# Where the splits of the next weights stand around the conditional part behind the last pair of experts

## The chip, the cores and the metric

The kernel runs on one core of a Trainium2 chip. The metric is the time of one execution on the device in microseconds, the median of the runs made; lower is better.

## What is computed

The reference is one transformer block with a mixture of experts, followed by two layers of a second kind. Cut to what stands around the change:

```python
h2 = rmsnorm(x, norm_ffn_g).reshape(b * s, d)          # 512 tokens, d = 1024
m = hierarchical_moe(h2, ...)                          # 2 of 32 experts for each token
x = rmsnorm(x + m, final_norm_g)                       # end of the first block

# second block, for l = 0, 1
h = rms_norm(x, norm_gain[l])
cols = h @ w_in                                        # layer 0: w_in_a (q, k, v, q_mem, gate)
kv = rms_norm(mem, mem_gain) @ w_mem_kv[l]             # memory: 256 rows, keys and values of layer l
```

## The kernel before

**The experts.** The 32 experts run as 16 pairs (a loop over j at L1468). For each pair 64 token slots are gathered for either expert, turned (`turn_tokens`), multiplied with the gate and up weights (`gate_up`, L1405), activated (`hidden`, L1410 to L1412), turned (`turned`, L1418 to L1420) and multiplied with the down weights (`down`, L1431). The output `y` leaves its two banks in halves: ScalarE copies the first (L1435), VectorE the second (L1433). GpSimd then scatters `y` into the DRAM tensor `yd` (L1436).

**The conditional part.** An expert with more than 64 tokens needs an extra pass. `extra(e)` (L1504) is written 14 times under nested conditions (L1549) on a count that is read at run time. With these data the count is zero and every engine branches over all 14 passes. Behind the branch each engine makes an entry on its own semaphore (and SP and GpSimd on those of their DMAs) for what the skipped code would have counted; in the trace these are the instructions of L1549 that are called EVENT_SEMAPHORE and INC_SWDGE_SEM. What another engine does behind the branch on a bank that the skipped code also uses waits for that entry.

**What follows.** `x2` holds four chunks of 128 tokens. To each, two tiles `m` read back from `yd` (L1563, L1564) are added (`add_experts`, L1566, L1567). TensorE transposes the chunks (`transposed`): chunk by chunk into six banks (three called sc, one oT, two tp) at L404, and then the last two slabs of 128 columns at L412 into sc banks that the first slabs have left. ScalarE and VectorE turn each slab into a pair `hh`, `hl` (L383, L384). Then the first projection of the new rows starts (`natural`, matmuls `sc<-whi,hh`). Besides, `square` (L1571) sums the squares of a chunk, `gF2` (L1559) is the squared gain, and both are used for the scale `R` of the rows.

**The fill.** The keys and values of the memory for layer 1 (`vB_steps` with `memory_steps`, and `mem_k`) need nothing of the experts. They are given to TensorE piece by piece (`pump`) around the additions and transposes. `mT` is the transposed memory, loaded by `mem_load` and split by `mem_split` (L641, L642). The value matmuls go into one bank sc and one bank oT, which `store_v` (L1457, output `vm`) empties.

**The weights.** All weights come through one `Stream` named `ws`, in the order of a plan. A unit is 128x1024 float32, 512 KB. `_load` (L217) is issued by SP as soon as one of three raw slots is free. `_split` writes `whi` with ScalarE (L229) and `wlo` with VectorE, every eighth time with GpSimd (L232), into one of five pairs of slots. Every matmul with weights is done three times (L370 hi with hi, L371 lo with hi, L372 hi with lo), which keeps the precision of float32. `ws.upto` is the index of the first unit that may not yet be split, and `ws.advance()` loads and splits as much as slots and `upto` allow. `own` is the index of the first unit behind the experts' weights. From there on the units are four of `w_mv` (values of the memory, layer 1), four of `w_mk` (keys) and then those of `w_va` (first projection of layer 0). I call them V1 to V4, K1 to K4 and A1, A2 and so on.

**What sets the order.** Inside `manual_schedule` the named engines keep the order in which the code is written: TensorE, ScalarE, VectorE and GpSimd around the last pairs and again behind the conditional part. SP's order, and that of all that is written outside of such blocks, is set by the scheduler, which fills gaps with it. Each engine then executes its queue strictly in order.

Of the kernel before, what the change touches and what calls it, by code (L numbers as in the profile page):

```python
# [16 lines left out]
AF = mybir.ActivationFunctionType  # L17
# [292 lines left out]
def build(tc, A, out, dbg=None):  # L310
# [3 lines left out]
    V, S, G, T = nc.vector, nc.scalar, nc.gpsimd, nc.tensor  # L314
# [8 lines left out]
    def acc():  # L323
        return ps.tile([128, 512], F32, name="acc", tag="acc", bufs=2)
# [245 lines left out]
    ws = Stream(nc, [(ap, "w") for ap in plan1 + kv0] + moe_u + [(ap, "w") for ap in plan2], ahead=3)  # L570
# [806 lines left out]
    def gather(j, ix):  # L1377

        nc.gpsimd.indirect_dma_start(out=xgs[j % 2], out_offset=None, in_=x1d,
                                     in_offset=bass.IndirectOffsetOnAxis(ap=ix, axis=0),  # L1380
                                     bounds_check=511, oob_is_err=False)
# [17 lines left out]
    def gate_up(get, X, p, us):  # L1399

        for u in us:
            w = [get(), get()]
            for k in range(2):
                for e, z in enumerate(sides):
                    T.matmul(p[z], X[2 * u + k][:, z], w[e][k], start=u + k == 0, stop=u + k == 4)  # L1405

    def hidden(p, hr, w):

        th = hchunk("th")[:, :256]
        S.activation(th, p[:, :256], AF.Tanh, scale=hr)  # L1410
        V.scalar_tensor_tensor(th, th, 1.0, p[:, :256], op0=OP.add, op1=OP.mult)
        V.scalar_tensor_tensor(th, th, w, p[:, 256:], op0=OP.mult, op1=OP.mult)  # L1412
        return th
# [51 lines left out]
    own = len(plan1) + 8 + 192  # L1465
    ws.upto = own
    pg, Xnext = acc(), None
    for j in range(-1, 16):  # L1468
        if j >= 0:
            th = hidden(pg, rw[:, j:j + 1], cw[:, j:j + 1])  # L1470
        if j < 15:
            Xg = Xnext or Xg
            pg = acc() if j >= 0 else pg
            gate_up(ws.get, Xg, pg, range(3))
        if j < 14:
            Xnext = turn_tokens(j + 2)
            if j < 12:
                gather(j + 4, idx[:, j + 4:j + 5])
        if j >= 0:
            t = turned(th)  # L1480
        if j < 15:
            gate_up(ws.get, Xg, pg, range(3, 4))
        if j >= 0:
            down(ws.get, t, odx[:, j:j + 1])
        if j == 0:
            pump(kv)
        if j == 13:
            mem2 = mem_load(mo)
        if j == 14:
            ws.upto = own + 2  # L1490
        if j == 13 and not dbg.get("noif"):
            nv = nc.values_load(next_i[0:1, 0:1], min_val=0, max_val=14)
    mT = mem_split(mo, mem2)
    ws.upto = own + 8
    ws.advance()
    order.close()
    vB_steps = memory_steps(ws, mT, store_v, (scp, otp))
# [54 lines left out]
    gF = bcast_row(mo, 0, 1024, "gF", "mraw", MR)  # L1552
# [3 lines left out]
    ms = []  # L1556
    gF2 = big("gF2", "mraw", MR)
    with tc.manual_schedule(engines={ET.PE, ET.Activation, ET.DVE, ET.Pool}):
        S.activation(gF2, gF, AF.Square)  # L1559
        kmB = [mo.tile([128, 512], F32, name="kmB", tag="mraw", bufs=MR) for _ in range(2)]  # L1560
        ms, ms2 = ([big("m", "mraw", MR) for c in range(4)] for _ in range(2))
        for c in range(4):
            nc.sync.dma_start(ms[c], yd[128 * c:128 * c + 128, :])  # L1563
            nc.sync.dma_start(ms2[c], yd[512 + 128 * c:640 + 128 * c, :])  # L1564
        def add_experts(c):
            V.tensor_tensor(x2[c], x2[c], ms[c], OP.add)  # L1566
            V.tensor_tensor(x2[c], x2[c], ms2[c], OP.add)  # L1567
            tap("x2", x2[c], c)

        def square(c):  # L1570
            S.activation(ms[c], x2[c], AF.Square, accum_out=s3[:, c:c + 1])  # L1571
        pump(vB_steps, AFTER[0])
        add_experts(0)
        pump(vB_steps, AFTER[1])
        add_experts(1)
        square(0)
        pump(vB_steps)
        kv = mem_k(1, mT, mo, lambda j: kmB[j])
        tps = [bank() for bank in (scp, scp, scp, otp, tpp, tpp)]

        def beside(c):
            if c != 1:
                pump(kv, AFTER[c + 2])
            if c in (0, 2):
                add_experts(2 + c // 2)
            if c == 3:
                ws.upto = own + 10
                ws.advance()
        hT = transposed(x2, gFA, hp_, "h", 16, tps=tps, more=scp, before=beside)
        ws.upto = None  # L1590
        for c in range(1, 4):
            square(c)
        for c in range(4):
            V.tensor_tensor_reduce(ms2[c], ms[c], gF2, 1.0, 0.0, OP.mult, OP.add, s4[:, c:c + 1])

        V.tensor_scalar(a12[:, 1], s3, 1.0 / 1024, EPS, OP.mult, OP.add)
        V.tensor_scalar(a12[:, 0], s4, 1.0 / 1024, None, OP.mult)
        V.scalar_tensor_tensor(a12[:, 0], a12[:, 1], EPS, a12[:, 0], op0=OP.mult, op1=OP.add)
        G.tensor_tensor(r12, a12, mhalf.rearrange("p (a c) -> p a c", a=2), OP.pow)
        pump(kv, 2)  # L1600
# [493 lines left out]
```

## Time and profile before

| | |
|---|---|
| median of 3 runs | 1861.84 us (1859.59 to 1862.24) |
| the profiled execution | 1861.34 us |
| its span, first to last instruction | 1859.6 us |
| TensorE busy | 97% of the span |
| mean granted clock of TensorE | 0.990 |

One execution was profiled. Times below are microseconds from the start of its span. Each engine has its own queue (PE is TensorE, DVE VectorE, ACT ScalarE, POOL GpSimd, SP issues most DMAs); a q behind the name marks instructions that only the queue's sequencer handles. In a row the bracket gives how long the engine was idle before it and what released it.

### The profile page before, as it was taken

Reading aid. Unit: us, or ns where it says so; the run is one execution under the profiler, and the core shown is the slowest. Engines: PE = TensorE matmul, PEld = TensorE weight load, DVE = VectorE, ACT = ScalarE, POOL = GpSimd, SP = SyncE. Lnnn points to the kernel's source line nnn. Section 1 sums busy time; section 2 is a strip of 40 time slices with the busy share of each in tenths; the row PEclk is TensorE's granted clock in tenths of the full one; section 3 lists DMA queues with packets and bytes.
Section 4 is the critical chain, followed back from the end, with each engine's and each line's share of the span. In section 5 each row is a group of like instructions: output and inputs, shape, how many; then the busy total and the mean of one; then the engine's idle time right before and its main releaser. Section 6 shows DMA issues by size and latency. Waiting matters only on the chain.

```text
span 1859.6 us, 25386 instructions
## 1 busy us (share of the span) xinstructions
PE 1797.6 (97%) x9466; PEld 1386.2 (75%) x9466; DVE 881.7 (47%) x1864; ACT 731.5 (39%) x1747; POOL 359.4 (19%) x461
## 2 busy tenths in 40 slices
PE   8999999999899886999999999999999999999999
PEld 8857776788533322798989799989788787777887
DVE  4389765365422112842443422342575336667571
ACT  5475355343101002534554424454563333233450
POOL 1301200011211101114424104524200002212210
PEclk9999999999999998999999999999999999999999
DMA  5221222178999998532311122311242332211231
GB/s 180 79 69 35 74 69 74 57 247 302 354 413 410 405 407 333 223 127 91 104 56 53 62 91 91 100 59 46 69 135 93 114 106 65 68 58 58 69 113 57
DMA packets 82787, 261.14 MB, mean 140 GB/s; under 512 B 11872, under 2 KB 13792, under 8 KB 82656
## 3 DMA queue, kind: packets, MB, share of 16 engines
q1 hardware_dynamic: 77184, 248.43, 37.8%
q0 software_dynamic: 4608, 8.40, 1.2%
q10 hardware_dynamic: 864, 2.62, 0.3%
q8 instruction: 76, 1.25, 0.3%
q14 instruction: 55, 0.45, 0.1%
HBM read 248.92 MB, written 18.87 MB: 144 GB/s over the span
## 4 chain that ended last, share of the span: by engine, by line
PE 57%; DVE 2%; ACT 1%; POOL 0%; issue 0%; DMA 0%; ACTq 0%; POOLq 0%; DVEq 0%
PE acc L370 14%; PE acc L371 13%; PE acc L372 13%; PE sc L370 2%; PE sc L372 2%; PE sc L371 2%; PE sc L1964 1%; PE sc L1760 1%; PE tp L1701 1%; PE sc L1763 1%; PE tp L1768 1%; PE oT L1777 1%; PE oT L2012 1%; DVE wlo L232 1%; ACT whi L229 0%; PE oT L1772 0%
## 5 line engine op out<-in xcount | busy, mean ns | idle before, releaser
L370 PE MATMUL acc<-whi,hh 128*128 128x512 f32 (+2 forms) x936 | 382.1, 410 | 1.4 <-ACT hh L383 0.6
L371 PE MATMUL acc<-wlo,hh 128*128 128x512 f32 (+2 forms) x936 | 371.7, 398 | 0.0
L372 PE MATMUL acc<-whi,hl 128*128 128x512 f32 (+2 forms) x936 | 371.2, 399 | 0.0
L232 DVE TENSOR_TENSOR wlo<-wraw,whi 128x1024 fp32r<-128x1024 f32 (+4 forms) x213 | 249.2, 1176 | 228.8 <-ACT whi L229 228.1
L229 ACT ACTIVATE whi<-wraw 128x1024 fp32r<-128x1024 f32 (+4 forms) x243 | 243.2, 1003 | 263.1 <-PE acc L371 112.7
L370 PEld LDWEIGHTS acc<-whi,hh 128*128 128x128 f32 x936 | 222.9, 238 | 27.7 <-issue 2.8
L371 PEld LDWEIGHTS acc<-wlo,hh 128*128 128x128 f32 x936 | 223.5, 239 | 22.4 <-issue 1.7
L372 PEld LDWEIGHTS acc<-whi,hl 128*128 128x128 f32 x936 | 222.5, 238 | 21.6
L370 PE MATMUL acc<-hh,whi 128*128 128x512 f32 x448 | 184.8, 412 | 0.3 <-DVE rsa L364 0.3
L372 PE MATMUL acc<-hh,wlo 128*128 128x512 f32 x448 | 177.7, 397 | 0.0
L371 PE MATMUL acc<-hl,whi 128*128 128x512 f32 x448 | 176.8, 395 | 0.0
L232 POOL TENSOR_TENSOR wlo<-wraw,whi 128x1024 fp32r<-128x1024 f32 (+3 forms) x30 | 69.1, 2305 | 528.4 <-ACT whi L229 441.5
L365 POOL TENSOR_TENSOR rs<-rsa,mhalf 128x4 f32<-128x4 f32 (+1 forms) x80 | 79.4, 992 | 328.4 <-DVE rsa L362 270.1
L713 ACT ACTIVATE hjk<-acc 128x128 bf16<-128x128 f32 x232 | 64.3, 277 | 104.2 <-PE acc L372 73.3
L370 PEld LDWEIGHTS acc<-hh,whi 128*128 128x128 f32 x448 | 84.5, 189 | 21.9 <-issue 5.6
L1405 PE MATMUL acc<-mraw,xgt 128*64 128x512 f32 x232 | 97.4, 618 | 3.3 <-DMA mraw<-in_w_moe 3.2
L372 PEld LDWEIGHTS acc<-hh,wlo 128*128 128x128 f32 x448 | 84.2, 188 | 19.8 <-issue 1.0
L371 PEld LDWEIGHTS acc<-hl,whi 128*128 128x128 f32 x448 | 84.5, 189 | 15.5
L716 DVE TENSOR_TENSOR nat<-acc,rs 128x512 f32<-128x512 f32 x52 | 35.9, 691 | 61.4 <-POOL rs L365 43.5
L1420 ACT ACTIVATE hid<-tp 128x256 f32<-128x256 f32 x16 | 6.1, 384 | 149.5 <-PE tp L1418 149.5
L1433 DVE COPY y<-sc 128x512 f32<-128x512 f32 x16 | 11.1, 692 | 107.3 <-PE sc L1431 107.3
L1392 DVE TENSOR_TENSOR xgt<-tp,c_vecs 128x512 f32<-128x512 f32 x32 | 20.6, 686 | 84.5 <-PE tp L1390 80.3
(539 smaller groups left out, 3179.4 us busy)
## 6 DMA issues: line engine op xcount, KB each, us to landing
mraw<-in_w_moe SPq DMA_DIRECT2D x86, 512.0 KB, 10.0
wraw<-in_w_qka SPq DMA_DIRECT2D x48, 512.0 KB, 3.9
xraw<-in_w_moe SPq DMA_DIRECT2D x25, 512.0 KB, 9.7
wraw<-in_w_va SPq DMA_DIRECT2D x24, 512.0 KB, 4.3
hraw<-in_w_moe SPq DMA_DIRECT2D x44, 256.0 KB, 9.6
praw<-in_w_moe SPq DMA_DIRECT2D x22, 512.0 KB, 9.8
qraw<-in_w_moe SPq DMA_DIRECT2D x21, 512.0 KB, 9.6
wraw<-in_w_qfb SPq DMA_DIRECT2D x16, 512.0 KB, 3.5
```

What stands on the lines that cost most here:

```text
L229: nc.scalar.activation(hi, raw, AF.Copy)
L232: eng.tensor_tensor(lo, raw, hi.bitcast(F32), OP.subtract)
L365: G.tensor_tensor(r[:, :m], t[:, :m], mhalf[:, :m], OP.pow)
L370: T.matmul(p, a[0], b[0], start=start, stop=False)
L371: T.matmul(p, a[0], b[1], start=False, stop=False)
L372: T.matmul(p, a[1], b[0], start=False, stop=stop)
L713: S.activation(jk, p[:, h * 128:h * 128 + 128], AF.Square, accum_out=st[:, h:h + 1])
L716: V.tensor_tensor(t.rearrange("p (h d) -> p h d", h=nh), p.rearrange("p (h d) -> p h d", h=nh), r[:, :nh, None].to_broadcast([128, nh, 128 ...
L1392: V.tensor_tensor(t.rearrange("p (k n) -> p k n", k=4), tp.rearrange("p (k n) -> p k n", k=4), vec(V_FFN + 4 * q, 4)[:, :, None].to_broadc ...
L1405: T.matmul(p[z], X[2 * u + k][:, z], w[e][k], start=u + k == 0, stop=u + k == 4)
L1701: T.transpose(tp[:, c * 128:c * 128 + 128], nat[c][:, j * 128:j * 128 + 128], ident)
L1760: T.matmul(p[32 * j:32 * j + 32, :256], q0[:, 128 * j + c:128 * j + 128:4], k0[:, 128 * BASE[j]:128 * BASE[j] + 256], start=True, stop=True)
```

## The change

At j == 14 the limit `ws.upto` is no longer raised, so no split stands among the work of the last pairs. Behind the loop the limit becomes `own + 2` instead of `own + 8`: only V1 and V2 may be split ahead of the conditional part by the written order. The limit `own + 8` and a call of `advance` come behind it. The square of the gain, `gF2`, moves from the front of that block to behind the transposes.

```diff
-        if j == 14:
-            ws.upto = own + 2
         if j == 13 and not dbg.get("noif"):
             nv = nc.values_load(next_i[0:1, 0:1], min_val=0, max_val=14)
     mT = mem_split(mo, mem2)
-    ws.upto = own + 8
+    ws.upto = own + 2
     ws.advance()
     order.close()
...
     gF2 = big("gF2", "mraw", MR)
     with tc.manual_schedule(engines={ET.PE, ET.Activation, ET.DVE, ET.Pool}):
-        S.activation(gF2, gF, AF.Square)
+        ws.upto = own + 8
+        ws.advance()
         kmB = [mo.tile([128, 512], F32, name="kmB", tag="mraw", bufs=MR) for _ in range(2)]
...
         hT = transposed(x2, gFA, hp_, "h", 16, tps=tps, more=scp, before=beside)
         ws.upto = None
+        S.activation(gF2, gF, AF.Square)
         for c in range(1, 4):
             square(c)
```

Line numbers behind the first lines of the diff are two smaller in the changed kernel, and one smaller behind its second part. The first place in the order of the instructions is VectorE in front of the conditional part. Before, from the activation of the last pair (`th`) to the branch:

```order
L1412 SCALAR_TENSOR_TENSOR th<-th,cw,acc 128x256
L232 TENSOR_TENSOR wlo<-wraw,whi 128x1024 x2
L1433 COPY y<-sc 128x512
L642 TENSOR_TENSOR mT<-mem,mT 128x1024 x2
L232 TENSOR_TENSOR wlo<-wraw,whi 128x1024 x2
L1549 COMPARE_AND_BRANCH
```

Changed:

```order
L1411 SCALAR_TENSOR_TENSOR th<-th,acc 128x256
L1412 SCALAR_TENSOR_TENSOR th<-th,cw,acc 128x256
L1433 COPY y<-sc 128x512
L642 TENSOR_TENSOR mT<-mem,mT 128x1024 x2
L232 TENSOR_TENSOR wlo<-wraw,whi 128x1024 x3
L1547 COMPARE_AND_BRANCH
```

Of five units that were split in front of the branch (the fifth by GpSimd) three are left: V1, V2 and V3, which the scheduler takes ahead of the branch by itself. They stand behind the copy of `y` and the lo halves of `mT`. V4 and K1 are loaded and split behind the branch.

The second place is SP's queue behind the branch. Before (the loads of V4, `wraw_6054`, and K1, `wraw_6060`, stand in front of the branch; 6089, 6095 and 6101 are K2 to K4):

```order
L1077 DMA gF_8632<-in_rows 128x1024
L217 DMA wraw_6089<-in_w_mk 128x1024
L217 DMA wraw_6095<-in_w_mk 128x1024
L217 DMA wraw_6101<-in_w_mk 128x1024
L1563 DMA m_8644<-yd_76 128x1024
L1564 DMA m_8648<-yd_76 128x1024
L1563 DMA m_8645<-yd_76 128x1024
L1564 DMA m_8649<-yd_76 128x1024
L1563 DMA m_8646<-yd_76 128x1024
L1564 DMA m_8650<-yd_76 128x1024
L1563 DMA m_8647<-yd_76 128x1024
L1564 DMA m_8651<-yd_76 128x1024
```

Changed, behind `gF` and the load of V4 (6083 is K1, 8627, 8633 and 8639 are K2 to K4):

```order
L1562 DMA m_8643<-yd_76 128x1024
L217 DMA wraw_6083<-in_w_mk 128x1024
L1563 DMA m_8647<-yd_76 128x1024
L1562 DMA m_8644<-yd_76 128x1024
L217 DMA wraw_8627<-in_w_mk 128x1024
L1563 DMA m_8648<-yd_76 128x1024
L1562 DMA m_8645<-yd_76 128x1024
L1563 DMA m_8649<-yd_76 128x1024
L1562 DMA m_8646<-yd_76 128x1024
L1563 DMA m_8650<-yd_76 128x1024
L217 DMA wraw_8633<-in_w_mk 128x1024
L217 DMA wraw_8639<-in_w_mk 128x1024
```

All of K2 to K4 stood ahead of the eight reads of `yd`; now K1 and K2 stand among them and K3 and K4 behind them.

The third place is ScalarE behind the branch. Before (8694 and 8715 are K3 and K4, 8811, 8817, 9033 are A1 to A3):

```order
L229 ACTIVATE whi_8694<-wraw_6095 128x1024
L1571 ACTIVATE m_8644,s3_8636<-x2_6104 128x1024
L229 ACTIVATE whi_8715<-wraw_6101 128x1024
L1457 ACTIVATE vm_8733<-sc_8660 128x512
L1457 ACTIVATE vm_8736<-oT_8661 128x512
L229 ACTIVATE whi_8811<-wraw_8678 128x1024
L229 ACTIVATE whi_8817<-wraw_8698 128x1024
L383 ACTIVATE hh_8829<-sc_8739,gFA_4535 128x512
L383 ACTIVATE hh_8833<-sc_8740,gFA_4535 128x512
L229 ACTIVATE whi_9033<-wraw_8719 128x1024
L383 ACTIVATE hh_8837<-sc_8741,gFA_4535 128x512
```

Changed (8693 and 8714 are K3 and K4, 8810, 8816, 9033, 9039 are A1 to A4):

```order
L229 ACTIVATE whi_8693<-wraw_8633 128x1024
L1570 ACTIVATE m_8643,s3_8618<-x2_6086 128x1024
L229 ACTIVATE whi_8714<-wraw_8639 128x1024
L1457 ACTIVATE vm_8732<-sc_8659 128x512
L1457 ACTIVATE vm_8735<-oT_8660 128x512
L229 ACTIVATE whi_8810<-wraw_8677 128x1024
L229 ACTIVATE whi_8816<-wraw_8697 128x1024
L229 ACTIVATE whi_9033<-wraw_8718 128x1024
L383 ACTIVATE hh_8828<-sc_8738,gFA_4535 128x512
L229 ACTIVATE whi_9039<-wraw_8814 128x1024
L383 ACTIVATE hh_8832<-sc_8739,gFA_4535 128x512
L383 ACTIVATE hh_8836<-sc_8740,gFA_4535 128x512
```

K3, the first square, K4 and the two `vm` keep their places to each other. A3 comes ahead of the first `hh` now, and A4 between the first and the second; VectorE's `wlo` and `hl` follow the same order.

## Rows read from the trace of the kernel before

**Rows 1.** The page's head: the span and its instructions.
```profile
span 1859.6 us, 25386 instructions
```

**Rows 2.** Busy time by stretch: stretch, length, engines, TensorE's granted clock, DMA share, GB/s.
```profile
core 0: us, PE busy (x) PEld busy (x) DVE busy (x) ACT busy (x) POOL busy (x), PEclk, DMA share, GB/s
513.80:517.30 3.50, 3.29 (x8) 0.99 (x10) 0.00 (x0) 0.00 (x0) 0.00 (x0) 0.51 1.05 405
612.80:619.60 6.80, 5.08 (x12) 1.65 (x14) 0.00 (x0) 0.96 (x2) 0.00 (x0) 0.50 1.02 408
732.30:742.50 10.20, 5.14 (x12) 4.12 (x13) 2.96 (x3) 3.17 (x3) 2.65 (x2) 0.50 0.76 274
767.30:1858.00 1090.70, 1083.02 (x6105) 926.38 (x6104) 510.05 (x984) 453.05 (x1115) 254.65 (x321) 1.00 0.26 84
```

**Rows 3.** TensorE in order of time: start, us, line, operation [idle before, releaser].
```profile
514.01 1.11 PE L1405 MATMUL acc<-xraw,xgt 128*64 128x512 f32 x1 [4.83 <-DMA xraw<-in_w_moe]
614.52 1.08 PE L1431 MATMUL sc<-hraw,hid 128*64 128x512 f32 x1 [5.51 <-DMA hraw<-in_w_moe]
726.22 2.36 PE L1431 MATMUL sc<-mraw,hid 128*64 128x512 f32 x9 [0.47 <-ACT hid L1420]
737.36 0.77 PE L370 MATMUL sc<-whi,mT 128*128 128x512 f32 x1 [7.49 <-DVEq L1549]
754.48 0.49 PE L404 MATMUL sc<-c_ident,x 128*128 128x128 f32 x3
767.32 0.50 PE L370 MATMUL sc<-whi,hh 128*128 128x512 f32 x1
```

**Rows 4.** Instructions of L1549: queue, operation, count: ns min/median/max, first and last start.
```profile
L1549 DVEq COMPARE_BRANCH  x1: 72/72/72, 734.3 to 734.3; - x1
L1549 POOLq INC_SWDGE_SEM  x1: 824/824/824, 736.4 to 736.4; - x1
L1549 DVEq EVENT_SEMAPHORE  x1: 21/21/21, 737.2 to 737.2; - x1
```

**Rows 5.** ScalarE, then VectorE, then GpSimd in order of time.
```profile
726.06 1.99 ACT L229 ACTIVATE whi<-wraw 128x1024 fp32r<-128x1024 f32 x2
728.28 0.60 ACT L1435 ACTIVATE y<-sc 128x512 f32<-128x512 f32 x1 [0.22 <-ACT whi L229]
...
733.16 2.25 ACT L229 ACTIVATE whi<-wraw 128x1024 fp32r<-128x1024 f32 x2 [1.45 <-DMA wraw<-in_w_mv]
...
750.51 0.60 ACT L1457 ACTIVATE vm<-sc 128x512 f32<-128x512 f32 x1 [0.79 <-PE sc L372]
...
763.13 1.27 ACT L383 ACTIVATE hh<-sc,gFA 128x512 fp32r<-128x512 f32 x2 [5.60 <-PE sc L404]
...
730.55 2.35 DVE L642 TENSOR_TENSOR mT<-mem,mT 128x1024 fp32r<-128x1024 f32 x2
...
763.85 1.41 DVE L384 SCALAR_TENSOR_TENSOR hl<-sc,gFA,hh 128x512 fp32r<-128x512 f32 x2 [4.53 <-ACT hh L383]
...
731.39 1.23 POOL L1436 DMA_INDIRECT yd<-y,v0o  x1 [5.25 <-ACT mT L641]
```

**Rows 6.** SP's queue in order of time: the DMAs that it issues.
```profile
728.40 0.33 SPq L217 DMA_DIRECT2D wraw<-in_w_mv  x1
...
735.34 2.85 SPq L217 DMA_DIRECT2D wraw<-in_w_mk  x3
738.42 0.33 SPq L1563 DMA_DIRECT2D m<-yd  x1
```

**Rows 7.** DMA in 742 to 757, at 758, at 731 us: issues, KB, us to landing.
```profile
DMA packets 1848, 6.22 MB, mean 415 GB/s; under 512 B 203, under 2 KB 203, under 8 KB 1848
...
wraw<-in_w_va SPq DMA_DIRECT2D x1, 512.0 KB, 4.0
...
yd<-y,v0o POOLq DMA_INDIRECT x1, 4.9
```

**Rows 8.** Groups by line and form in 726 to 790 us: busy, mean ns | idle before.
```profile
L229 ACT ACTIVATE whi<-wraw 128x1024 fp32r<-128x1024 f32 x16 | 16.8, 1057 | 11.0 <-PE oT L372 4.3 <-DMA wraw<-in_w_va 3.6 <-PE acc L372 1.6
L232 DVE TENSOR_TENSOR wlo<-wraw,whi 128x1024 fp32r<-128x1024 f32 x13 | 15.6, 1221 | 10.6 <-ACT whi L229 10.5
L1567 DVE TENSOR_TENSOR x<-x,m 128x1024 f32<-128x1024 f32 x4 | 4.9, 1226 | 0.2
L384 DVE SCALAR_TENSOR_TENSOR hl<-sc,gFA,hh 128x512 fp32r<-128x512 f32 x5 | 3.6, 745 | 4.5 <-ACT hh L383 4.5
```

## The prediction

> **What bounds the kernel now.** The profiled execution took 1861.34 us, of which 1859.6 us are its span [rows 1] and 1.74 us lie around it; it stands 0.5 us under the median of the three runs, 1861.84 us. I read the sums by stretch first. Behind the stage that is changed, from 767.3 us to the end, TensorE is busy 1083 of 1090.7 us at a granted clock of 1.00 [rows 2]. So nothing behind it can take up a delay: what this stage loses or gains is lost or gained for the whole kernel. I then read the stage itself in the order of time, engine by engine. TensorE ends the last pair of experts and stands still for 7.49 us until 737.36 us; what releases it is VectorE's entry at L1549, the conditional part [rows 3]. That part is skipped with these data. VectorE branches at 734.3 us and makes its entry for the skipped code at 737.2 us, 2.9 us later; GpSimd ends its own at 736.4 + 0.82 = 737.2 us [rows 4]. From 732.3 to 742.5 us the granted clock is 0.50 (1.2 GHz), so the first 12 matmuls take 5.1 us [rows 2]. From 737.36 us on TensorE runs nearly without a hole: chunk 1 of the new x is transposed from 754.48 us, and the first matmul on the normed rows hh starts at 767.32 us [rows 3]. That last time is the one I forecast.
>
> The pieces of weights that count are V1 to V4 (w_mv), K1 to K4 (w_mk) and A1 to A4 (w_va), 512 KB each, every one loaded into one of three raw slots and split into hi and lo by ScalarE and VectorE (the eighth by GpSimd).
>
> **Part 1: in front of the branch.** Before, V1 and V2 are split ahead of the copy of the first half of y. They cost next to nothing there: ScalarE does both in 726.06 to 728.05 us and copies at 728.28 us [rows 5], while TensorE only starts the eight matmuls of that half at 726.22 us and needs about 2.1 us for them (nine in 2.36 us [rows 3]). So "output copies first" gains 0 to 0.2 us at this copy, and TensorE is then still busy on the second half. The two splits now stand behind the copies: on VectorE 3 x 1.22 us behind the two lo halves of mT instead of 2 x 1.22 us. Before, V4 and K1 stood among the splits ahead of the branch, and V4 was split only from 733.16 us, when it had landed [rows 5]; now all three inputs are there early. VectorE ends mT at 730.55 + 2.35 = 732.9 us [rows 5]; three lo behind it, started 1.14 us apart, end near 736.3 us, and ScalarE, which is ahead of it, ends their hi near 733.7 us. The branch can go between 733.7 us (when the last lo is handed over) and 735.1 us (when it starts); with the 2.9 us of before the entry comes at 736.6 to 738.0 us. Against 737.2 us that is -0.6 to +0.8 us; I take -0.5 us. It leads nowhere, though, because TensorE then meets the later waits below: it goes into the length of those, not into the sum.
>
> **Part 2: the loads.** The splits of V1 and V2 free the raw slots in which V4 and K1 are loaded. Before, these two loads were issued from 728.40 us on, in front of the branch, and then K2 to K4 from 735.34 us on ahead of the eight reads of yd (m), the first at 738.42 us [rows 6]. In the changed order SP issues behind the branch gF, V4, m, K1, m, m, K2, five m, K3, K4. gF and V4 can go when TensorE's entry and the first lo are there (732 to 734 us). The first m needs the scatter of y, issued at 731.39 us [rows 5] and landed 4.9 us later [rows 7], and GpSimd's entry: not before 736.3 us, and not later than the 738.42 us of before. I take the end of that entry, 737.2 us. From it to K4 there are twelve transfers. A lone one takes 4.0 us from issue to landing; in a full stretch the core moves 415 GB/s, 512 KB in 1.26 us [rows 7]. So K3, the eleventh, lands at 737.2 + 4.0 + 10 x 1.26 = 753.8 us and K4 at 755.1 us. Before, ScalarE never waited for them: what it waited for ahead of the vm copies was TensorE [rows 5].
>
> The Trainium skill (DMA: Bandwidth & Descriptors, Anatomy of one DMA) gives a DMA 2.0 us plus its bytes over 436 GB/s, an estimate of 3.2 us for 512 KB. The row here says 4.0 us; by the page both lone landings in this sum would come 0.8 us earlier and the sum would be some 0.8 to 1.6 us smaller, inside the range below.
>
> **Part 3: who waits for K3 and K4.** ScalarE's order is strict: split K3, square of x (chunk 0), split K4, then the two copies vm that empty the banks sc and oT. Before, the first ran at 750.51 us, held by TensorE alone [rows 5]. Now: K3 753.8 us, square 754.75 us, K4 755.85 us, vm at 756.8 and 757.5 us, the second done at 758.1 us (splits of 1.06 us, started about 1 us apart [rows 8]). The transposes of chunk 0 need both banks: the fourth of them, into oT, can't start before 758.1 us. VectorE says the same: lo of K3 until 756.1 us, then two additions of 1.23 us for chunk 1 [rows 8] until 758.6 us; TensorE transposes chunk 1 then, against 754.48 us before [rows 3]. **First stall: 4.1 us.** All that follows is moved by it; hh of the first slab comes at 767.2 instead of 763.13 us [rows 5].
>
> **Part 4: the hole behind the transposes.** In the new order ScalarE splits A4 between the first and the second hh, and VectorE does lo of A4 between the first and the second hl; before, both second halves came first. A4's raw slot is freed by the lo of A1, which VectorE does behind all additions: lo of K4 until 759.7 us, chunk 2 until 762.1 us, chunk 3 until 764.5 us, A1 until 765.65 us. The load is issued at 765.7 us and lands 4.0 us later, 769.7 us. Then whi 1.06, lo 1.22, hl 0.75 us (the second hh runs beside the lo) [rows 8]: the second hl is done at 772.7 us. Before, two hl in a row were done at 763.85 + 1.41 = 765.3 us [rows 5]. TensorE's second slab of transposes and all behind it wait for that: **+7.4 us** in all, the first 4.1 us included.
>
> gF2 is moved behind the hh. It costs ScalarE 1.06 us there and finds cover: two splits that stood among the hh are gone from there, and the scale R, which TensorE takes up after some 13 us of matmuls, keeps 2 us or more to spare. Were that gone, the price would be the 1.06 us.
>
> **Clock.** A hole of 4.83 us at 514.01 us was followed by 0.51 of the clock until 517.3 us, one of 5.51 us at 614.52 us by 0.50 until 619.6 us [rows 2, 3]. The first stall is 4 to 5 us long, so I expect the same: half of 3.3 to 5.1 us lost, 1.6 to 2.5 us. Most of it falls into the second wait, which is set by A4 and not by TensorE: with hh 2.5 us later, A4 is split at 770.4 instead of 769.7 us. I take 0.5 us; 0 to 0.7 us here, and up to 1.7 us more if the second hole lowers the clock again.
>
> **Sum.** 7.4 + 0.5 = 7.9 us: 1861.34 + 7.9 = 1869.2 us against the profile's own time, and 1869.7 us at the median's level. The bounds: first m at 736.3 us (-0.9) or 738.4 us (+1.2), clock 0 to 2.4 us: 1868.3 to 1873 us.
>
> **Rivals.**
> 1. Not slower. If K3 and K4 came in time for the vm copies, only the front would show: the entry up to 0.6 us earlier, and the slow clock ended sooner (12 matmuls at 0.43 instead of 0.23 us are 2.3 us). That is 1859 to 1862 us, 1860.5 us say. It decides at K4's landing: it would have to be there by about 749 us, a split ahead of the vm copies of before, which leaves 7.8 us behind the first landing for eleven transfers that take 13.9 us at the rate of the rows. Against it stands also that the first of them can't start before y is scattered. 8%, of which 3% by more than 0.2% faster.
> 2. Only the first stall. If A4 is there before its turn (VectorE done with the additions sooner, or the second wait covered), 4.1 us stay, and the clock's 1.6 to 2.5 us are then paid in full: 1866.0 to 1868.4 us. For it speaks that A4's load before was issued well ahead of its split; against it that its slot now waits for ten VectorE operations in a row. 16%.
> 3. Both stalls and two falls of the clock, and the first m as late as before: 1873 to 1876 us. 9%.
> 4. The change doesn't do what it says: the third split is in front of the branch, by the scheduler, so the front is nearly as long as before and the first gap stays above 7 us. This is contained in the forecast, since the front drops out of the sum.
>
> **How the numbers follow.** Forecast 67%, rivals 8, 16 and 9%. The range takes in rival 2 and leaves out rival 1 and most of 3: 1865.5 to 1873.5 us. A measurement of this kernel can tell about 0.2%, 3.7 us, from no change. Slower by more: the forecast, rival 3 and nearly all of 2, 0.88; within: 0.09; faster: 0.03.
>
> **What would show it.** In the profile after: idle of TensorE before the third or fourth transposes at L404 of 3 to 5 us, released by ScalarE's vm, with ScalarE waiting for K3's load; a second hole before the second slab, released by hl, behind a wait for A4; a clock of 0.50 behind the first. Were the L404 transposes reached without a wait, the loads are faster than I think and the forecast is wrong; were there a first hole and no second, rival 2 holds.

## The result: 11 us slower, and the profile after

The changed kernel takes 1871.68 us, the median of 4 runs (1870.88 to 1872.33), against 1860.71 us before (4 runs, 1858.63 to 1862.24). The ratio is 1.0059, with an interval of 1.0042 to 1.0077, which is 7.8 to 14.3 us. The forecast was 1869.7 us in a range of 1865.5 to 1873.5 us. The profiled execution took 1870.88 us. Its span is 9.5 us longer than that of [rows 1]; it is the fastest of the four, 0.8 us under their median, and the profiled one of before stands 0.6 us over its own, so the medians lie 1.4 us further apart than the two profiles.

The last expert matmuls start at 727.37 us here and at 726.22 us before [rows 3]. These 1.15 us come from far ahead: at the first matmuls of the last pairs, near 692 us, the two executions already stand 1.04 us apart. In the later runs this start lies anywhere from 724.45 to 729.85 us. So I compare the stage from its own entry on, which is the first matmul `sc<-whi,mT` behind the conditional part, to the first matmul on hh.

TensorE in order of time, after (start, us, line, operation, idle before and releaser), as in [rows 3]:

```profile
738.61 0.77 PE L370 MATMUL sc<-whi,mT 128*128 128x512 f32 x1 [7.58 <-DVEq L1547]
...
755.02 0.38 PE L404 MATMUL sc<-c_ident,x 128*128 128x128 f32 x2
760.60 0.47 PE L404 MATMUL sc<-c_ident,x 128*128 128x128 f32 x1 [5.19 <-ACT vm L1457]
...
761.79 0.90 PE L404 MATMUL sc<-c_ident,x 128*128 128x128 f32 x3
...
773.12 0.66 PE L412 MATMUL sc<-c_ident,x 128*128 128x128 f32 x4 [1.02 <-DVE hl L384]
775.38 0.66 PE L412 MATMUL sc<-c_ident,x 128*128 128x128 f32 x4 [1.60 <-DVE hl L384]
```

The gap at the conditional part has hardly changed (7.58 against 7.49 us). New are a stall of 5.19 us in the middle of chunk 0's transposes, released by the copy vm, and one of 1.60 us in the middle of the L412 transposes. The 1.02 us in front of those were there before as well; then all eight ran in one piece:

```profile
764.65 1.31 PE L412 MATMUL sc<-c_ident,x 128*128 128x128 f32 x8 [1.02 <-DVE hl L384]
```

The first matmul on hh starts at 777.27 us, 38.66 us behind the entry, against 29.96 us before (767.32 - 737.36). That is +8.70 us.

Busy time by stretch, after (columns as in [rows 2]):

```profile
757.35:764.18 6.83, 3.57 (x13) 2.89 (x14) 6.00 (x6) 5.68 (x8) 0.00 (x0) 0.50 0.65 188
...
776.80:1868.00 1091.20, 1083.16 (x6107) 926.62 (x6105) 510.47 (x982) 451.98 (x1113) 255.26 (x321) 1.00 0.26 83
```

Behind the first stall the granted clock is 0.50 (1.2 GHz). Behind the stage TensorE is as full as before and takes nothing up: from the first matmul on hh to the end of the span it is 1091.83 us, against 1092.28 us before. So the span's 9.5 us are 1.15 ahead of the stage, 0.10 at the entry, 8.70 in the stage and -0.45 behind it.

What the first stall waits for is read from ScalarE in order of time, after:

```profile
745.60 1.06 ACT L229 ACTIVATE whi<-wraw 128x1024 fp32r<-128x1024 f32 x1 [5.33 <-DMA wraw<-in_w_mk]
749.43 1.06 ACT L229 ACTIVATE whi<-wraw 128x1024 fp32r<-128x1024 f32 x1 [2.76 <-DMA wraw<-in_w_mk]
757.02 1.06 ACT L229 ACTIVATE whi<-wraw 128x1024 fp32r<-128x1024 f32 x1 [6.53 <-DMA wraw<-in_w_mk]
757.98 1.04 ACT L1570 ACTIVATE m<-x 128x1024 f32<-128x1024 f32 x1
...
759.02 1.04 ACT L229 ACTIVATE whi<-wraw 128x1024 fp32r<-128x1024 f32 x1
759.97 0.57 ACT L1457 ACTIVATE vm<-sc 128x512 f32<-128x512 f32 x1
760.45 0.58 ACT L1457 ACTIVATE vm<-oT 128x512 f32<-128x512 f32 x1
...
771.59 0.69 ACT L383 ACTIVATE hh<-sc,gFA 128x512 fp32r<-128x512 f32 x1 [3.66 <-PE sc L404]
772.34 1.06 ACT L229 ACTIVATE whi<-wraw 128x1024 fp32r<-128x1024 f32 x1
```

The first three rows are K1, K2 and K3. ScalarE stands 6.53 us for K3's load. Behind K3 follow the square, K4 and the two vm, one after the other; before, the first vm waited for TensorE alone [rows 5]. SP's queue (start, us, line, DMA) and the chain of waits (start, us, what) show why K3 is late:

```profile
738.62 0.33 SPq L1562 DMA_DIRECT2D m<-yd  x1
739.04 0.66 SPq L217 DMA_DIRECT2D wraw<-in_w_mk  x1
...
745.54 0.32 SPq L1563 DMA_DIRECT2D m<-yd  x1
746.87 2.63 SPq L217 DMA_DIRECT2D wraw<-in_w_mk  x2
```

```profile
732.53 5.81 DMA yd<-y,v0o
...
739.81 7.00 DMA m<-yd
746.87 10.04 DMA wraw<-in_w_mk
...
759.97 0.58 ACT vm L1457
760.60 0.47 PE sc L404
```

K3 is issued at 746.87 us, behind the eight reads of yd, and lands 10.04 us later. What SP waits for just before is the landing of the read issued at 739.81 us (739.81 + 7.00), eight DMAs earlier in its queue. Before, it was issued with K2 and K4 from 735.34 us on, ahead of all reads [rows 6].

### The profile page after: what moved, and what is told of

The parts are those of the page before. It is cut to its first block, busy times and chain, and to the rows that moved or that the text cites. A ratio compares the mean times of both kernels' runs of the same rounds, so it can differ in the third digit from the quotient of the medians.

```text
span 1869.1 us, 25379 instructions
## 1 busy us (share of the span) xinstructions
PE 1799.1 (96%) x9466; PEld 1387.9 (74%) x9466; DVE 883.5 (47%) x1864; ACT 730.9 (39%) x1747; POOL 360.4 (19%) x461
## 3 DMA queue, kind: packets, MB, share of 16 engines
q8 instruction: 76, 1.25, 0.3%
## 4 chain that ended last, share of the span: by engine, by line
PE 85%; DMA 9%; DVE 3%; ACT 2%; issue 1%; POOL 0%; SPq 0%; ACTq 0%; POOLq 0%; DVEq 0%
PE acc L370 19%; PE acc L371 18%; PE acc L372 18%; PE acc L1405 3%; DMA mraw<-in_w_moe 3%; PE sc L370 3%; PE sc L371 3%; PE sc L372 3%; PE sc L1964 1%; PE sc L917 1%; PE sc L1760 1%; DMA xraw<-in_w_moe 1%; PE sc L1431 1%; PE tp L1701 1%; PE oT L942 1%; DMA hraw<-in_w_moe 1%
## 5 line engine op out<-in xcount | busy, mean ns | idle before, releaser
L371 PEld LDWEIGHTS acc<-hl,whi 128*128 128x128 f32 x448 | 84.5, 189 | 15.4
```

Source lines behind the costliest of these rows:

```text
L371: T.matmul(p, a[0], b[1], start=False, stop=False)
```

## The experiments

Each kernel was measured against the kernel before. "Entry to hh" is in microseconds, from the one execution of each kernel that was profiled; "us more" is the ratio times 1861 us, with the ratio's interval. I name them in words; the table holds what is used below.

| kernel | entry to hh | us more than before |
|---|---|---|
| before | 29.96 | |
| after | 38.66 | 11.0 (7.8 to 14.3) |
| after, SP in the written order | 35.24 | 7.3 (4.8 to 9.9) |
| after, A3 and A4 behind all hh | 35.92 | 9.5 (6.9 to 12.1) |
| both | 32.00 | 4.3 (2.6 to 6.0) |
| after, two reads of yd instead of eight | 33.12 | 3.7 (2.0 to 5.4) |
| after, order mended | 29.83 | 1.1 (-0.4 to 2.8) |
| before, only copies first | 38.52 | 7.4 (5.2 to 9.5) |
| before, only splits behind the branch | 42.40 | 10.8 (8.6 to 13.0) |
| before, only gF2 moved | 29.75 | 1.5 (-0.2 to 3.2) |
| after, gF2 back in front | 40.81 | 13.0 (10.4 to 15.4) |

### Which wait costs what

My theory: K3's place in SP's queue makes the first stall, A4's place on ScalarE and VectorE the second. Against it stands that splits behind the branch cost this wherever they stand, by their number or by the slow clock there.

SP in the written order, so that K1 to K4 are loaded ahead of the reads:

```diff
-    with tc.manual_schedule(engines={ET.PE, ET.Activation, ET.DVE, ET.Pool}):
+    with tc.manual_schedule(engines={ET.PE, ET.Activation, ET.DVE, ET.Pool, ET.SP}):
```

> The changed kernel with SP held to the written order in the stage behind the branch: V4, K1 to K4, then the eight reads m. The orders of ScalarE and VectorE are those of the changed kernel, word for word. Theory (K3 and K4 land late because they queue behind the reads m): the first stall before the transposes into the sc bank, 5.2 us in the changed kernel, falls to 1 us or less and the first matmul on hh comes 5 to 6 us earlier; the second hole (A4) stays at 1.5 to 3 us; total 2 to 4 us above the kernel before instead of 11. Rival (it is the splits of V4 and K1 themselves, moved behind the branch, that ScalarE and VectorE can't do in time, whatever the order of the loads): the stall stays above 4 us and the total within 2 us of the changed kernel.

A3 and A4 split behind all hh:

```diff
         hT = transposed(x2, gFA, hp_, "h", 16, tps=tps, more=scp, before=beside)
+        ws.upto = own + 12
+        ws.advance()
         ws.upto = None
```

> The changed kernel with the splits of A3 and A4 written behind all eight hh and hl; SP's order up to K4 unchanged. Theory: the first stall of 5.2 us and the low clock behind it stay as they are; the second hole of 1.6 us (and the wait of 1.0 us in front of the first slab of the last two) goes, so the first matmul on hh comes 2.5 to 3 us earlier: 8 to 9 us above the kernel before. Rival (the second hole only takes up what the first stall left, hh would come late anyway): within 1 us of the changed kernel.

Both:

> Both: SP in the written order (K1 to K4 ahead of the reads m) and A3, A4 behind all hh. All other parts of the change stay: copies first, V4 and K1 split behind the branch, gF2 behind the transposes. Theory: both stalls gone, nothing left of the loss: 0 to 1.5 us above the kernel before. Rival (work moved behind the branch, not its order, is the loss): 4 us or more above it.

TensorE in order of time, of these three in turn, and of the first SP's queue:

```profile
759.00 0.33 PE L404 MATMUL sc<-c_ident,x 128*128 128x128 f32 x1 [0.42 <-ACT vm L1457]
...
773.82 0.97 PE L412 MATMUL sc<-c_ident,x 128*128 128x128 f32 x4 [3.02 <-DVE hl L384]
```

```profile
740.40 8.68 SPq L217 DMA_DIRECT2D wraw<-in_w_mk  x4
749.32 0.33 SPq L1562 DMA_DIRECT2D m<-yd  x1
```

```profile
762.22 0.33 PE L404 MATMUL sc<-c_ident,x 128*128 128x128 f32 x1 [3.71 <-ACT vm L1457]
...
775.21 1.31 PE L412 MATMUL sc<-c_ident,x 128*128 128x128 f32 x8 [1.02 <-DVE hl L384]
```

```profile
756.26 0.33 PE L404 MATMUL sc<-c_ident,x 128*128 128x128 f32 x1 [1.63 <-ACT vm L1457]
...
767.40 1.31 PE L412 MATMUL sc<-c_ident,x 128*128 128x128 f32 x8 [1.02 <-DVE hl L384]
...
788.78 0.44 PE L703 MATMUL tp<-c_ident,mkn 128*128 128x128 f32 x2 [1.06 <-DVE mkn L716]
```

Each edit takes away the wait that it was aimed at. With K3 ahead of the reads the first stall falls from 5.19 to 0.42 us, although the clock behind the branch is as slow (0.53 in the first 5.1 us, 0.52 in the changed kernel's first 5.3) and the splits are as many. With A4 behind the hh the L412 transposes run in one piece again. Of the 2.7 us by which that stage is shorter, though, 1.5 us are a shorter first stall (3.71 us), which this edit doesn't touch: with the same order in SP's queue K3 lands 16.7 us behind the entry here and 18.3 us in the changed kernel.

The waits are not independent either. The written order of SP gives 3.4 us of the stage back and not the 5 to 6 that I expected, because SP stands at K4's load until GpSimd has done the lo of K1 and freed its slot (the row of 8.68 us), so the reads begin only at 749.32 us, the additions and A4 come late, and the second hole grows to 3.02 us; the clock is 0.53 from there to the first matmul on hh. With both edits the stage is still 2.0 us longer than before, with 1.63 us of the first stall left.

Behind the stage, the two kernels that split A3 and A4 later lose time again: from the first matmul on hh to the end of the span they take 1094.0 and 1093.4 us, the changed kernel 1091.8 us. A hole of 1.06 us at L703 is new in both; A3 and A4 now stand ahead of the squares and of gF2, which is the likely reason. In total both edits give back 6.7 of 11.0 us, less than I had expected, and what A4's place alone costs the whole kernel is not shown: 9.5 us (6.9 to 12.1) can't be told from 11.0 us (7.8 to 14.3). (In these three executions nine of the last expert matmuls took 3.9 to 4.0 us instead of 2.36 us; that lies ahead of the entry and is not in the stage.)

Less traffic, with the order of the changed kernel kept. This kernel leaves out six of the eight reads, and all four chunks add the rows of the last one:

```diff
-        for c in range(4):
+        for c in range(3, 4):
             nc.sync.dma_start(ms[c], yd[128 * c:128 * c + 128, :])
...
-            V.tensor_tensor(x2[c], x2[c], ms[c], OP.add)
-            V.tensor_tensor(x2[c], x2[c], ms2[c], OP.add)
+            V.tensor_tensor(x2[c], x2[c], ms[3], OP.add)
+            V.tensor_tensor(x2[c], x2[c], ms2[3], OP.add)
```

> The changed kernel with two reads m instead of eight; all four chunks add the rows of the last one, so the sums of the other three chunks are left wrong (six transfers of 512 KB less, the same additions). Orders otherwise as in the changed kernel. Theory: K3 and K4 land 7 us earlier, the first stall of 5.2 us goes with its low clock; the hole at A4 stays at 1 to 3 us. From TensorE's entry to the first matmul on hh 31.5 to 34 us instead of 38.7; total 2 to 5 us above the kernel before. Rival (not the transfers but the splits behind the branch hold ScalarE): the stall stays above 4 us.

TensorE in order of time:

```profile
753.82 0.49 PE L404 MATMUL sc<-c_ident,x 128*128 128x128 f32 x3
...
764.65 0.66 PE L412 MATMUL sc<-c_ident,x 128*128 128x128 f32 x4 [1.02 <-DVE hl L384]
766.73 0.94 PE L412 MATMUL sc<-c_ident,x 128*128 128x128 f32 x4 [1.42 <-DVE hl L384]
```

With six reads less in front of K3 it lands 9.1 us behind the entry instead of 18.3 us, and the transposes run through; nothing else in the order is changed. The hole that A4 makes remains, at 1.42 us, with a granted clock of 0.58 behind it, and the stage is 3.2 us longer than before. Together with the written order of SP this shows the first stall from both sides: it is the reads in front of K3, whether they are moved or left out.

The order mended, all else as in the changed kernel. SP: V4, K1, K2, two reads, K3, two reads, K4, four reads. A3 behind the last hh, A4 behind the squares:

```diff
-    with tc.manual_schedule(engines={ET.PE, ET.Activation, ET.DVE, ET.Pool}):
-        ws.upto = own + 8
+    with tc.manual_schedule(engines={ET.PE, ET.Activation, ET.DVE, ET.Pool, ET.SP}):
+        ws.upto = own + 3
         ws.advance()
...
         for c in range(4):
+            if c:
+                ws.upto = own + (4, 8, 8)[c - 1]
+                ws.advance()
             nc.sync.dma_start(ms[c], yd[128 * c:128 * c + 128, :])
...
-        ws.upto = None
+        ws.upto = own + 11
+        ws.advance()
         S.activation(gF2, gF, AF.Square)
...
+        ws.upto = None
         pump(kv, 2)
```

> The changed kernel with all of its moved work where the change put it (copies first, V4 and K1 split behind the branch, gF2 behind the transposes), and only the order behind the branch mended: SP issues V4, K1, K2, two m, K3, two m, K4, four m; A3 is split behind the hh, A4 behind the squares and sums. Theory (order is the whole loss): from TensorE's entry to the first matmul on hh 29.5 to 31 us, as in the kernel before (30.0); no hole of more than 0.5 us in front of the transposes nor behind the hh; total 0 to 2 us above the kernel before. Rival (a part of the loss is the work itself behind the branch): stage of 32 us or more, total 3 us or more above.

TensorE in order of time:

```profile
755.52 0.49 PE L404 MATMUL sc<-c_ident,x 128*128 128x128 f32 x3
...
766.35 1.31 PE L412 MATMUL sc<-c_ident,x 128*128 128x128 f32 x8 [1.02 <-DVE hl L384]
...
787.77 0.44 PE L703 MATMUL tp<-c_ident,mkn 128*128 128x128 f32 x2 [1.09 <-DVE mkn L716]
```

Neither stall is left (the 1.02 us were there before), the stage is 29.83 us long, and no difference to the kernel before can be measured. So splits behind the branch cost the stage nothing by themselves: the order of the loads and splits is its whole loss. In the whole kernel the interval leaves up to 2.8 us open, and a hole of 1.09 us at L703 remains, which I had not expected.

### The parts of the change alone

Only the copies first (taken from the kernel before):

```diff
-        if j == 14:
-            ws.upto = own + 2
```

> The kernel before without the raise of the limit at j == 14, and nothing else of the change: V1 and V2 are split behind the output copies and mT, the limit own + 8 and gF2 stay where they were. The order shows what follows from it: V4 and K1, though written ahead of the branch, fall behind it; SP issues V4, K1, K2, then the eight reads m, then K3 and K4; A3 comes ahead of the first hh and A4 behind it. Theory (order of SP and the place of A4 make the loss): K3 is the ninth transfer behind the first m instead of the eleventh, so the stall before the transposes is 1 to 4 us instead of 5.2, the hole at A4 stays; 4 to 8 us above the kernel before. Rival (putting the output copies first is harmless or good, the loss is in the limit of own + 2 behind the loop): within 1.5 us of the kernel before.

Only the limit behind the loop:

```diff
-    ws.upto = own + 8
+    ws.upto = own + 2
     ws.advance()
...
         S.activation(gF2, gF, AF.Square)
+        ws.upto = own + 8
+        ws.advance()
```

> The other half alone: V1 and V2 are split ahead of the copies as in the kernel before, but the limit behind the loop is own + 2 and own + 8 comes behind the branch; gF2 stays in front. The order: nothing is split behind mT in front of the branch; V3 waits behind gF2; all eight reads m stand ahead of K2, K3 and K4. Theory: VectorE branches about 2.4 us earlier than in the kernel before and TensorE resumes 1 to 2.4 us earlier, and it is of no use: K3 is the tenth transfer behind the first m, the stall before the transposes is 4 us or more, and the total is 6 to 11 us above the kernel before. Rival (the front bounds: what ends the first gap is what counts): 1 to 3 us below the kernel before.

TensorE in order of time, first copies first, then the limit; the latter's instructions of the branch (count: ns, start); and SP's loads of K3 and K4, and of K2 to K4, in the two:

```profile
758.80 0.48 PE L404 MATMUL sc<-c_ident,x 128*128 128x128 f32 x1 [2.92 <-ACT vm L1457]
```

```profile
736.64 0.76 PE L370 MATMUL sc<-whi,mT 128*128 128x512 f32 x1 [6.65 <-DVEq L1549]
...
757.90 0.66 PE L404 MATMUL sc<-c_ident,x 128*128 128x128 f32 x2 [4.24 <-DVE x L1569]
```

```profile
L1549 DVEq COMPARE_BRANCH  x1: 72/72/72, 730.9 to 730.9; - x1
...
L1549 DVEq EVENT_SEMAPHORE  x1: 21/21/21, 736.5 to 736.5; - x1
```

```profile
745.01 1.62 SPq L217 DMA_DIRECT2D wraw<-in_w_mk  x2
```

```profile
743.48 2.31 SPq L217 DMA_DIRECT2D wraw<-in_w_mk  x3
```

Either part alone makes most of the loss, 7.4 and 10.8 us, and both together make 11.0 us. That they don't add up fits that they do the same: in either kernel K3 is issued behind the eight reads (from 745.01 and 743.48 us on), as in the changed one. The second part empties the front best: VectorE branches at 730.9 us, 3.4 us earlier than before [rows 4]. Its entry comes at 736.5 us, only 0.7 us earlier, and TensorE gives that away at the transposes.

gF2, first moved in the kernel before, then moved back in the changed one (SP's order changes with it, and in the second that of the splits too):

```diff
-        S.activation(gF2, gF, AF.Square)
         kmB = [mo.tile([128, 512], F32, name="kmB", tag="mraw", bufs=MR) for _ in range(2)]
...
         ws.upto = None
+        S.activation(gF2, gF, AF.Square)
```

> The kernel before with only gF2 moved behind the transposes. The order shows that SP then issues K2, m, K3, m, m, K4, five m; the orders of VectorE and of the splits among the hh stay (both first halves hh ahead of A3). Theory: K3 is the second and K4 the fifth transfer from the first m on, both there several us before TensorE is through with the values, so no stall comes in front of the transposes; gF2 among ScalarE's later work is covered: within 1.5 us of the kernel before. Rival (gF2's place or any m ahead of a K load costs): 2 us or more above.

> The changed kernel with gF2 back at its old place, in front of the stage. The scheduler's order shows more than that: with gF2 ahead of it, V3's split stays behind the branch, V4 and K1 are loaded ahead of the reads m, K2 to K4 behind all of them, and A3 and A4 are both split ahead of the first hh. Theory: the entry of VectorE comes about 2.4 us earlier (5.2 instead of 7.6 us idle), which leads nowhere; K3 is the tenth transfer behind the first m instead of the eleventh, so the stall ends up to 2 us earlier; A4 holds the first hh instead of the second. Total 8 to 11 us above the kernel before. If gF2's place itself were the loss (1.06 us of ScalarE among the hh), the total would fall by 1 us and the rest stay as in the changed kernel.

The move makes no difference that can be measured, 1.5 us (-0.2 to 3.2). Moved back it makes the changed kernel no faster: the stage takes 40.81 us, with a wait of 4.09 us for the additions in front of chunk 0 and 1.86 us for vm. 13.0 us more than before (10.4 to 15.4) lies above the 8 to 11 us that I expected, though the interval reaches into them.

### Can the gap at the branch be used?

If the branch costs TensorE 7.5 us with the splits behind it or in front, can other matmuls fill it? Here the kernel before gets the first 25 value matmuls ahead of the branch, and A3 and A4 later:

```diff
+    vB_steps = memory_steps(ws, mT, store_v, (scp, scp))
+    pump(vB_steps, 4)
+    xbank = scp()
     order.close()
-    vB_steps = memory_steps(ws, mT, store_v, (scp, otp))
...
-        pump(vB_steps, AFTER[0])
+        pump(vB_steps, AFTER[0] - 4)
```

> Built on the kernel before: the first matmuls of the memory's values (25 by the order: V1, V2 and one of V3) are placed in front of the branch, into two sc banks that the conditional passes leave alone (those passes use one sc bank for both halves); A3 is split behind the hh, A4 behind the squares and sums. Theory (the gap behind the last pair is the latency of the branch, and only work of TensorE in front of it can use it): TensorE starts on them when mT is split, about 2 to 3 us behind its last expert matmul, and branches behind them; with a clock of 1.00 it is through with V1 and V2 by 738 us and resumes at 740 to 742 us with 23 matmuls left: 2 to 5 us below the kernel before. If the clock falls as it did there, all 25 run at half speed and the branch comes late: 0 to 1 us below. Rival (its own branch, now late, adds its whole latency behind the matmuls): 1 to 3 us above.

The next kernel takes that one, puts four reads of yd ahead of K2 to K4, and the vm copies ahead of the K splits. With it gF is loaded behind the reads and gF2 comes behind the hh, and SP keeps the written order:

```diff
         for c in range(4):
+            if c == 2:
+                ws.advance()
             nc.sync.dma_start(ms[c], yd[128 * c:128 * c + 128, :])
...
-        square(0)
         pump(vB_steps)
+        ws.upto = own + 8
+        ws.advance()
+        square(0)
```

> The kernel with the matmuls of V1, V2 in front of the branch, and behind it SP's order mended to what TensorE then needs: four m, K2 to K4, four m, gF; the copies vm ahead of the splits of K2 to K4; gF2 behind the hh. Theory: in the kernel that only filled the gap TensorE reached the transposes 7 us early and waited 4.0 us for the additions of chunk 0 and 2.2 us for vm; here the first m is issued at about 737.5 us and the second landed by 743 us, so the additions are done at 745.5 us, when TensorE is through with the values: the two holes fall to 1 us together, one or two waits of 1 to 2 us come for K2 and the additions of chunk 2. First matmul on hh 3 to 6 us earlier than before, counted from the last expert matmuls; total 2 to 5 us below the kernel before. Rival (the reads m can't start before TensorE's own entry, and twelve transfers need 18 us from there, whatever the order): the time is moved behind the transposes of chunk 2 or 3, total within 1.5 us of the kernel before.

The last one also issues the stores of vm behind the loads of A1 to A5:

```diff
         S.activation(t, p, AF.Copy)
-        nc.sync.dma_start(kvd[:, 1024 + 512 * c:1536 + 512 * c], t)
+        late.append((c, t))
...
+                for j, t in late:
+                    nc.sync.dma_start(kvd[:, 1024 + 512 * j:1536 + 512 * j], t)
```

> The kernel with the matmuls in front of the branch and the mended order (e10_m), with the two stores of vm issued behind the loads of A1 to A5 instead of ahead of A1. In e10_m TensorE reached the transposes of chunk 3 3.5 us earlier than in the kernel before, counted from the last expert matmuls, and then waited 5.3 us for the first hl, which ScalarE held back for A1 and A2 (landed 764.0 and 765.2 us, behind the stores). Theory: A1 lands 3 to 5 us earlier, the hole of 5.3 us falls to 1 to 2 us, the first matmul on hh comes 2 to 4 us earlier than in the kernel before; total 2 to 4 us below it. Rival (the loads of A1 and A2 are late because their raw slots come late and eight m and gF are in front of them, not because of the stores): the hole stays above 3.5 us, total within 1.5 us of the kernel before or above.

TensorE in order of time, of the three in turn:

```profile
731.72 0.50 PE L372 MATMUL sc<-whi,mT 128*128 128x512 f32 x1 [1.25 <-DVE mT L642]
...
749.95 0.30 PE L404 MATMUL sc<-c_ident,x 128*128 128x128 f32 x1 [3.99 <-DVE x L1569]
...
752.47 0.96 PE L404 MATMUL sc<-c_ident,x 128*128 128x128 f32 x2 [2.22 <-ACT vm L1457]
```

```profile
768.36 1.97 PE L412 MATMUL sc<-c_ident,x 128*128 128x128 f32 x8 [5.28 <-DVE hl L384]
```

```profile
763.09 1.31 PE L412 MATMUL sc<-c_ident,x 128*128 128x128 f32 x8 [2.72 <-DVE hl L384]
```

The gap of 7.5 us is down to 1.25 us, and yet the first of the three is 3.2 us slower than before (1.5 to 4.7), the second 2.2 (0.4 to 3.9) and the third equal (-0.4, -2.0 to 1.3). I had expected gains from all three. From the start of the last expert matmuls to the first on hh they take 42.87, 43.50 and 40.09 us, the kernel before 41.10 us. The gap only moves: TensorE comes to chunk 0 earlier and waits there for the additions (3.99 us), and with the reads first it waits for hl (5.28 and 2.72 us), since ScalarE and VectorE are held by A1 and A2, whose loads come late. The place of the stores accounts for a part: with them behind the loads the hole falls from 5.28 to 2.72 us, not to the 1 to 2 us that I expected. My reading is that the one queue of transfers and VectorE, through which everything between the scatter of y and hh runs, set the length of the stage; no run here tests that by itself. No version was measurably faster than the kernel before.

## Why the prediction was right, point by point

**Behind the stage** nothing took the delay up, as said from [rows 2]: -0.45 us of 8.70.

**Part 1, the front.** VectorE does branch earlier, 7.43 us behind the start of the last expert matmuls instead of 8.08 us, as forecast. But its entry came 3.6 us behind the branch and not 2.9 us as in [rows 4]. So TensorE gained nothing, +0.10 us instead of -0.5. The step that failed is the carrying over of the 2.9 us; as argued, it led nowhere.

**Part 2, the loads: the mis-sized term.** I compare with the forecast moved by the 1.15 us of drift. The first read is issued at 738.62 us (forecast 738.35) and lands after 3.2 us, at 741.8 us. That is 0.5 us early, since this transfer took 3.2 us instead of the 4.0 us of [rows 7]. Its DMA issue and that of A4's load, used in part 4 (KB, us to landing):

```profile
m<-yd SPq DMA_DIRECT2D x1, 512.0 KB, 3.2
```

```profile
wraw<-in_w_va SPq DMA_DIRECT2D x1, 512.0 KB, 3.4
```

The estimate from the Trainium skill (DMA: Bandwidth & Descriptors, Anatomy of one DMA — SWDGE (gpsimd) path), 3.2 us for 512 KB, meets this one landing, though the skill states that fit for DMAs that GpSimd issues, and SP issues this one. In the kernel that only splits A3 and A4 later the same read took 4.9 us. From there the transfers should have followed each 1.26 us. K1, the second, came 3.7 us behind the first, at 745.52 us; from K1 to K3 there are nine steps of 1.27 us, as forecast. So K3 landed at 756.92 instead of 754.95 us, 1.97 us late, all of it from one slow start. The stretches show it (columns as in [rows 2]):

```profile
738.60:741.20 2.60, 2.60 (x6) 2.12 (x7) 0.89 (x1) 1.06 (x1) 0.00 (x0) 0.50 0.63 205
741.20:743.90 2.70, 2.70 (x8) 2.08 (x8) 0.34 (x1) 0.00 (x0) 0.00 (x0) 0.54 0.88 209
743.90:757.00 13.10, 11.50 (x51) 9.03 (x49) 3.59 (x3) 2.12 (x2) 2.39 (x1) 1.00 1.02 414
```

The queue moves 205 to 209 GB/s until 743.9 us and 414 GB/s behind it. In the kernel before it moved 397 GB/s then:

```profile
738.40:743.90 5.50, 5.50 (x17) 4.35 (x16) 0.03 (x1) 2.12 (x2) 0.00 (x0) 0.62 1.01 397
```

Nor does the order alone make it: the kernel that only splits A3 and A4 later has the same order in SP's queue, and there 335 GB/s were moved in the 5.3 us from its first read on. K3 landed 17.5 us behind that read's issue, against 18.3 us here and 16.6 us in the sum. Why it starts slowly here stays open; no run was aimed at it.

**Part 3, who waits.** Right in mechanism and in size from K3's landing on: 4.11 us to the end of the second vm (756.92 to 760.45 + 0.58), 4.3 forecast. Chunk 1 is transposed 6.06 us later behind the entry, 4.1 us forecast; the difference is K3's 1.97 us.

**Part 4, the second hole.** The additions end 2.0 us later than the sum said, at 767.66 us. A4's load takes 3.4 us instead of 4.0 us, the chain behind it 3.1 us as forecast (3.0), and the second hl is done at 775.33 us, 1.5 us later than said. So this wait moves the L412 transposes by 8.8 us instead of 7.4 us.

**The clock.** It fell as expected, to 0.50 for 6.8 us, and its loss of about 2 us lies in the wait for A4 as forecast: A4 landed at 772.26 us, just as the first hh ended (771.59 + 0.69). Its own share in the sum is near zero instead of 0.5 us. Since the two ended together, the trace doesn't show which of them set the split of A4.

**The sum.** The sum of the stage was 7.4 + 0.5 = 7.9 us and measured 8.7 us. That it is so close is in part luck: K3's 2.0 us too many are met by 0.6 us less for A4's load and 0.5 us less for the clock. The total's 11.0 us has an interval that holds both. Of the 2.3 us over 8.7 us, 1.4 us are the distance of the two profiled executions from their medians and 0.8 us lie outside of the stage in these two; whether any of that belongs to the change, no run settles.

**gF2** has its cover, as said: no hole behind the hh in the changed kernel.

**The rivals.** K4 in time (rival 1) would have needed a landing at 749 us; it came at 758.15 us. Only the first stall (rival 2) is excluded by the 1.60 us at L412. A second fall of the clock (rival 3) did not come in the changed kernel. Behind the hole at L412 the clock did fall in four others: in SP in the written order and with two reads, where no first stall had lowered it, and in either part of the change alone. That the third split stays in front and the first gap over 7 us (rival 4) was right, 7.58 us, and inside the forecast.

## What to carry to other kernels

Work that is moved behind a point takes its loads with it, and the place of those loads in the one queue that issues them decides the time: list the queue in its new order, count what stands ahead of the first piece that an in-order engine splits before it empties a bank, and the stall can be sized before anything runs, here to about 2 us. With loads and splits put in the order in which they are used, and still behind the branch, 11.0 us fell to 1.1 us, which is no measurable difference. Filling a gap with other matmuls gained nothing measurable here in three versions: TensorE then waited for additions and hl instead. Look first at what sets the start of the next stage.

## What the runs showed of the hardware

- **The skipped code has no fixed price.** From VectorE's branch to its entry it took 2.9 us before and 3.6 us after, and between 2.8 and 5.6 us in the other kernels. It was longest where VectorE branched earliest (5.6 us from 730.9 us on), though it doesn't follow that order throughout. The entry stayed 9.7 to 12.3 us behind the start of the last expert matmuls in all of them. What sets it was not tried.
- **A transfer of 512 KB** took 3.2 us from issue to landing as the first read of yd and 3.4 us as the load of A4, 6.5 us as the second in a slow queue (K1) and 10.0 us behind seven others (K3), of which only 1.27 us is its own turn.
- **The clock after a hole** fell to 0.50 behind holes of 2.92 to 5.28 us in this stage (behind one of 3.71 us only after 1.8 us at 0.92). Below that it went both ways: behind 1.02 and 1.42 us with four transposes between, the kernel with two reads had 0.58 in the 1.7 us that followed, while the changed kernel had 1.00 behind 1.02 and 1.60 us, and the last of the three that fill the gap 1.00 behind 2.72 us.
